# A decoder layer whose whole down projection goes by seven half-size products, with partial sums kept in PSUM or added in DRAM

## The chip, the cores and the metric

The kernel runs on one core of a Trainium2 chip. The metric is the device time of one execution in microseconds (us), in fp32, with inputs and outputs in DRAM. TensorE (PE) multiplies, VectorE (DVE) and ScalarE (ACT) do the rest of the arithmetic, GpSimd (POOL) only issues DMAs here, and SyncE (SP) issues most of the DMAs.

## The reference

One decoder layer over 512 tokens of width 2048: a mixer (attention heads beside a state-space scan), a cross-attention and an MLP, each with a residual. What the change touches is the last line and, through the weights' buffers, everything from `w_out` on:

```python
x = x + jnp.concatenate([attn, ssm], axis=-1) @ w_out[i]
x = x + cross_attention(rms_norm(x, g_cross[i]), rms_norm(mem, g_mem[i]), ...)
hm = rms_norm(x, g_mlp[i])
x = x + jnp.square(jax.nn.relu(hm @ w_up[i])) @ w_down[i]     # 2048 -> 8192 -> 2048
```

## The kernel before

Every large product is made of three TensorE products of a reduced fp32 type: each operand is split into a high part (an ACT copy) and a low part (a DVE subtraction), and high by high, high by low and low by high are added in PSUM. `weights` (L203 on) splits a plain 512 KB weight block; it takes 24 matmuls of 512 columns.

The up projection uses a scheme with seven products of half-size blocks in place of eight (Winograd's form). `up_forms` (L894) makes from one 512 KB block three raw quarters and four sums (DVE, L901 to L904), splits all seven (ACT L899 and L905, DVE L908 and L909); `forms` (L855) does the like for the activations. `up_products` (L916) runs 42 matmuls of 256 columns for such a block, into four PSUM banks, and `combine` (L924) makes the four result blocks from the seven sums. `up_out` (L941) applies the squared ReLU and writes the hidden rows to DRAM (`adr`).

The down projection goes over the 8192 hidden rows in NC = 8 chunks of 1024. In each chunk the first DS = 1024 output columns go by seven products (four column blocks S0 to S3 of 256, two weight blocks each), the other 1024 plainly (P0 and P1 of 512, four weight blocks each): 16 steps in a chunk, half of either kind. `mm_step` (L1089) takes four fresh banks for each column block, from the tags "mm" and "aux" in turn (eight banks in all), so that one block is emptied while the next is multiplied. `evac_step` (L1108) empties them: plain blocks by DVE into `acc` in SBUF (L1117), seven-product blocks by an ACT copy in the first chunk (L1130) and DVE additions after that (L1128), into `accs` in SBUF. `a_load`, `a_split` and `a_forms` (L1132 to L1145) load hidden rows and make their forms; `cols_sum` and `cols_out` (L1147 on) combine at the end, transpose on PE (L1158), add the residual `x3d` from DRAM (L1159) and store.

Order: from the mixer's end to L1050 parts are in an order written by hand; the up and down loops are placed by the compiler's scheduler, by priority in program order. Each engine and each DMA queue runs its own list in order. SBUF: the pool `wp` holds three raw weight blocks (WR) and two high and two low ones (WH) for the whole kernel; the mixer's scratch pool `bq` (12 tiles of 2 KB a partition, written by `ssd`, L589) is closed at L663, and `wq` (sums and their splits) opened on its bytes; 68 general tiles of 2 KB (`big`) hold activations. The first product after the mixer is `gemm_rows(cat, wout[0])` (called behind L682), whose first eight activation tiles are the attention's, ready before the last `ssd`.

## Time and profile before

| | us |
|---|---|
| median of 3 runs | 2353.99 (2353.25 to 2354.26) |
| profiled execution, whole | 2353.13 |
| its span, first to last instruction | 2351.1 |
| PE busy in the span | 2338.1 (99%) |
| DVE / ACT / POOL busy | 1686.9 / 1118.5 / 13.4 |

By place in the span: the mixer to about 690 us, the output projection to 906, cross-attention to 1015, the up projection from there to about 1667, the down projection to the end. A row of a group of instructions gives busy time, the mean duration of one in ns, and the idle time of its engine just before them with what ended it. Durations overlap by some 0.08 us from one instruction to the next on DVE and by more on PE; what an instruction costs in a full engine is the distance between starts.

### The profile page before, as it was taken

To read this page: it belongs to the slowest core of one execution; us is meant where nothing else is said; L and a number is where in the kernel's file an instruction comes from. 1 tells how busy PE (TensorE), PEld (TensorE's weight loads), DVE (VectorE), ACT (ScalarE), POOL (GpSimd) and SP (SyncE) were. 2 spreads that over 40 slices of the span, in tenths; PEclk is the share of its full clock that TensorE was granted. 3 is DMA by queue.
4 is the path that set the end of the run, shared out by engine and by line. 5 is a ranking of instruction groups with operands and counts; after the bars stand their busy time and mean duration, and the time that the engine had idled before them with its cause. 6 is when DMAs were issued, how large, how long until landed. Compare 5 with 4: busy or idle time off the path is not lost.

```text
span 2351.1 us, 36723 instructions
## 1 busy us (share of the span) xinstructions
PE 2338.1 (99%) x14606; PEld 2077.8 (88%) x14606; DVE 1686.9 (72%) x3100; ACT 1118.5 (48%) x1722; POOL 13.4 (1%) x30
## 2 busy tenths in 40 slices
PE   9999999999999999999999999999999999999999
PEld 8889977777778887789999999999988989889898
DVE  7544276686673346688888888888867887887787
ACT  6334277655452346675444444554543443443332
POOL 0000000000000000000000000000000000000000
PEclk9999999999999999999999999999999999999999
DMA  5222321122224456434443444444543433343344
GB/s 198 90 87 80 99 66 59 54 72 81 74 81 133 160 167 202 135 108 135 133 128 129 132 135 135 131 131 135 187 137 119 140 127 109 132 135 119 117 135 144
DMA packets 98283, 286.22 MB, mean 122 GB/s; under 512 B 11200, under 2 KB 15424, under 8 KB 98112
## 3 DMA queue, kind: packets, MB, share of 16 engines
q1 hardware_dynamic: 82368, 252.42, 33.3%
q10 hardware_dynamic: 13824, 25.17, 2.8%
q0 software_dynamic: 1920, 6.29, 0.9%
q8 instruction: 114, 1.87, 0.3%
q14 instruction: 57, 0.47, 0.1%
HBM read 254.48 MB, written 29.36 MB: 121 GB/s over the span
## 4 chain that ended last, share of the span: by engine, by line
PE 95%; ACT 2%; DVE 2%; issue 1%; DMA 0%; SPq 0%; ACTq 0%; DVEq 0%
PE mm L214 13%; PE mm L212 13%; PE mm L213 13%; PE aux L922 7%; PE mm L922 7%; PE aux L920 7%; PE mm L920 7%; PE aux L921 7%; PE mm L921 7%; PE aux L213 3%; PE aux L214 3%; PE aux L212 3%; PE aux L248 1%; PE aux L523 1%; PE aux L514 1%
## 5 line engine op out<-in xcount | busy, mean ns | idle before, releaser
L208 DVE TENSOR_TENSOR wl<-wr,wh 128x1024 fp32r<-128x1024 f32 (+2 forms) x223 | 264.4, 1186 | 281.7 <-ACT wh L207 280.9
L207 ACT ACTIVATE wh<-wr 128x1024 fp32r<-128x1024 f32 (+2 forms) x223 | 229.3, 1028 | 458.3 <-PE mm L214 250.3
L212 PE MATMUL mm<-wh,b 128*128 128x512 f32 (+2 forms) x1056 | 404.8, 384 | 3.3 <-ACT b L422 1.6
L213 PE MATMUL mm<-wl,b 128*128 128x512 f32 (+2 forms) x1056 | 402.8, 382 | 0.9 <-DVE wl L208 0.7
L214 PE MATMUL mm<-wh,b 128*128 128x512 f32 (+2 forms) x1056 | 402.6, 381 | 0.0
L899 ACT ACTIVATE wh<-wr 128x768 fp32r<-128x768 f32 x192 | 162.5, 846 | 309.4 <-PE mm L921 121.4
L909 DVE TENSOR_TENSOR sl<-sw,sh 128x1024 fp32r<-128x1024 f32 x192 | 234.5, 1221 | 97.1 <-ACT sh L905 96.8
L905 ACT ACTIVATE sh<-sw 128x1024 fp32r<-128x1024 f32 x192 | 203.6, 1061 | 120.3 <-DVE sw L904 37.1
L212 PEld LDWEIGHTS mm<-wh,b 128*128 128x128 f32 x1056 | 198.7, 188 | 42.9 <-ACT b L422 2.0
L213 PEld LDWEIGHTS mm<-wl,b 128*128 128x128 f32 x1056 | 198.8, 188 | 39.8 <-DVE wl L208 2.1
L214 PEld LDWEIGHTS mm<-wh,b 128*128 128x128 f32 x1056 | 198.7, 188 | 38.1 <-issue 0.2
L921 PE MATMUL mm<-b,sh 128*128 128x256 f32 x768 | 217.2, 283 | 0.0
L921 PE MATMUL aux<-b,sh 128*128 128x256 f32 x768 | 217.2, 283 | 0.0
L920 PE MATMUL mm<-b,sh 128*128 128x256 f32 x768 | 217.2, 283 | 0.0
L920 PE MATMUL aux<-b,sh 128*128 128x256 f32 x768 | 217.2, 283 | 0.0
L922 PE MATMUL mm<-b,sl 128*128 128x256 f32 x768 | 216.9, 283 | 0.0
L922 PE MATMUL aux<-b,sl 128*128 128x256 f32 x768 | 216.6, 283 | 0.0
L908 DVE TENSOR_TENSOR wl<-wr,wh 128x768 fp32r<-128x768 f32 x192 | 183.3, 955 | 26.9 <-ACT wh L899 19.8
L922 PE MATMUL aux<-b,wl 128*128 128x256 f32 x576 | 162.1, 282 | 1.2 <-DVE wl L908 1.1
L920 PE MATMUL mm<-b,wh 128*128 128x256 f32 x576 | 162.4, 282 | 0.0
L920 PE MATMUL aux<-b,wh 128*128 128x256 f32 x576 | 162.2, 282 | 0.0
L922 PE MATMUL mm<-b,wl 128*128 128x256 f32 x576 | 162.1, 281 | 0.0
(303 smaller groups left out, 5252.2 us busy)
## 6 DMA issues: line engine op xcount, KB each, us to landing
wr<-in_wup_dram SPq DMA_DIRECT2D x128, 512.0 KB, 3.8
wr<-in_wdp_dram SPq DMA_DIRECT2D x64, 512.0 KB, 3.7
wr<-in_wds_dram SPq DMA_DIRECT2D x64, 512.0 KB, 3.7
wr<-in_wzx_dram SPq DMA_DIRECT2D x48, 512.0 KB, 3.6
wr<-in_wout_dram SPq DMA_DIRECT2D x32, 512.0 KB, 3.8
a<-b ACTq DMA_DIRECT2D x64, 256.0 KB, 4.6
b<-a SPq DMA_DIRECT2D x64, 256.0 KB, 4.4
wr<-in_wqk_dram SPq DMA_DIRECT2D x31, 512.0 KB, 3.6
```

Of the source, the lines that this page charges most:

```text
L207: act.activation(hi, raw, AF.Copy)
L208: dve.tensor_tensor(lo, raw, hi.bitcast(F32), OP.subtract)
L212: pe.matmul(ps, l[0], r[0], start=start, stop=False)
L213: pe.matmul(ps, l[0], r[1], start=False, stop=False)
L214: pe.matmul(ps, l[1], r[0], start=False, stop=stop)
L899: act.activation(hi[:, :768], raw[:, 256:], AF.Copy)
L905: act.activation(shi, sw, AF.Copy)
L908: dve.tensor_tensor(lo[:, :768], raw[:, 256:], hi[:, :768].bitcast(F32), OP.subtract)
L909: dve.tensor_tensor(slo, sw, shi.bitcast(F32), OP.subtract)
L920: pe.matmul(ps[b][:, H], w[0][:, d], xf[0], start=st, stop=False, skip_group_check=True)
L921: pe.matmul(ps[b][:, H], w[0][:, d], xf[1], start=False, stop=False, skip_group_check=True)
L922: pe.matmul(ps[b][:, H], w[1][:, d], xf[0], start=False, stop=sp_, skip_group_check=True)
```

## The change

All 2048 columns of the down projection go by seven products: eight column blocks j of 256, two steps each, 16 steps in a chunk as before. Odd chunks take the columns in the reverse order; the last two blocks of a chunk stay in PSUM and go on in the next chunk. The other finished blocks are copied to SBUF by ACT, and DMAs from POOL write them to DRAM (`accd`), from the second time on with an addition there; for the last chunk they are loaded back (`acc_load`) and combined, and the last two blocks (LATE) are added on DVE. The residual is written straight to `out`, and the results are added to it there by DMAs from POOL. The seven sums are made with other signs, of the weights in three DVE instructions for four; in `up_products` the three products with raw quarters come first. The last two blocks of the up projection are interleaved. Weight buffers of the mixer (`wp`) are closed with it, and a pool `zp` is opened behind it, with four raw blocks.

```diff
-    wp = ctx.enter_context(tc.tile_pool(name="wp", bufs=2))
...
     bq = mixer.enter_context(tc.tile_pool(name="bq", bufs=NBUFQ))
+    wp = mixer.enter_context(tc.tile_pool(name="wp", bufs=2))
+    weight_tile = {"raw": lambda: wp.tile([128, 1024], F32, name="wr", tag="wr", bufs=WR), ...
...
     mixer.close()
-    wq = ctx.enter_context(tc.tile_pool(name="wq", bufs=WQ, reuse_waits="tile"))
+    zp = ctx.enter_context(tc.tile_pool(name="zp", bufs=2, reuse_waits="tile"))
+    weight_tile.update(raw=lambda: zp.tile([128, 1024], F32, name="zr", tag="zr", bufs=WZ),
+                       hi=lambda: zp.tile([128, 1024], F32R, name="zh", tag="zh", bufs=WH),
+                       lo=lambda: zp.tile([128, 1024], F32R, name="zl", tag="zl", bufs=WH))
...
-            act.dma_start(x3d[t, n], xr[t])
+            act.dma_start(out[t * 128:t * 128 + 128, n * 512:n * 512 + 512], xr[t])
...
+    prods = ((5, 4, 0, H0), (6, 5, 1, H0), (4, 0, 3, H0), (3, 3, 2, H0), (2, 2, 2, H1), (1, 1, 1, H1), (0, 6, 0, H1))
...
+        sw = zp.tile([128, 1024], F32, name="sw", tag="sw", bufs=WH)
+        rhi = zp.tile([128, 768], F32R, name="rh", tag="rh", bufs=WH)
+        rlo = zp.tile([128, 768], F32R, name="rl", tag="rl", bufs=WH)
+        shi, slo = weight_tile["hi"](), weight_tile["lo"]()
...
+        act.activation(rhi, q(raw, 0, 3), AF.Copy)
+        dve.tensor_tensor(h3(q(sw, 2, 2), 2), h3(q(raw, 0, 2), 2), q(raw, 3)[:, None, :].to_broadcast([128, 2, 256]), OP.add)
+        dve.tensor_tensor(q(sw, 1), q(sw, 2), q(raw, 1), OP.add)
+        dve.tensor_tensor(q(sw, 0), q(sw, 1), q(raw, 2), OP.add)
+        dve.tensor_tensor(rlo, q(raw, 0, 3), rhi.bitcast(F32), OP.subtract)
+        act.activation(shi, sw, AF.Copy)
+        dve.tensor_tensor(slo, sw, shi.bitcast(F32), OP.subtract)
...
+        for part in (prods[:3], prods[3:]):
+            for d in range(2):
+                for wi, xi, b, H in part:
...
+        dve.tensor_tensor(h3(t1, 2), h3(b[1], 2), p1[:, None, :].to_broadcast([128, 2, 256]), OP.add)
+        dve.tensor_tensor(h3(t2, 2), h3(b[2], 2), t1[:, None, H1].to_broadcast([128, 2, 256]), OP.add)
+        dve.tensor_tensor(t1[:, H1], b[0][:, H1], t2[:, H1], OP.add)
+        stt_(t3[:, H0], t2[:, H0], b[2][:, H1])
+        stt_(t3[:, H1], t2[:, H0], b[3][:, H0])
...
+    steps = [("U", 0, f, q, 4) for q in range(4) for f in (NU - 2, NU - 1)]
+    US = len(steps)
+    js = [list(range(NJ))[::1 - c % 2 * 2] for c in range(NC)]
+    steps += [("S", c, j, q, FCH // 512) for c in range(NC) for j in js[c] for q in range(FCH // 512)]
+    stays = {(c, j) for c in range(NC - 1) for j in js[c][-2:]}
...
+        fresh = q == 0 and (c - 1, j) not in stays
+        if fresh:
             tags[0] += 1
-            banks[kind, c, j] = [bank("mm" if tags[0] % 2 else "aux") for _ in range(4)]
+            banks[kind, j] = [bank("mm" if tags[0] % 2 else "aux") for _ in range(4)]
...
+            for b, w in enumerate(BW):
+                o = big()
+                act.activation(o[:, w], ps[b][:, w], AF.Copy)
+                if j in written:
+                    nc.gpsimd.dma_start(accd[j][b], o[:, w], accum_op=OP.add)
                 else:
-                    act.activation(accs[j][b][:, w], ps[b][:, w], AF.Copy)
+                    nc.gpsimd.dma_start(accd[j][b], o[:, w])
...
+        dve.tensor_tensor(h3(f1, 2), h3(ta, 2), tb[:, None, H1].to_broadcast([128, 2, 256]), OP.subtract)
+        stt_(f2[:, H0], f1[:, H0], ta[:, H1])
+        stt_(f2[:, H1], f2[:, H0], tb[:, H0])
+        a, b, f, g = split(ta), split(tb[:, H0], 256), split(f1), split(f2)
...
+            for k, o in enumerate((a, b)):
+                pe.transpose(p[:, 256 * i + 128 * k:256 * i + 128 * k + 128], o, ident)
+            act.activation(r[:, h], p[:, h], AF.Copy, scale=c2[:, t:t + 1])
+            nc.gpsimd.dma_start(out[t * 128:t * 128 + 128, j * 256:j * 256 + 256], r[:, h], accum_op=OP.add)
...
+        for p, (l, f) in enumerate(((-6, -4), (-5, -3), (-3, -1), (-2, 0)) if c == 0 else ((-15, -14), (-12, -11), (-9, -8), (-6, -5))):
+            task(b + l, a_load, c, p)
+            task(b + f, a_forms, c, p)
...
+        load_step(i + WZ - 1)
+        prep_step(i + 1)
+        if 0 < i <= len(steps):
             evac_step(i - 1)
+        for t in tasks.get(i, ()):
+            t[0](*t[1:])
+        if i < len(steps):
             mm_step(i)
...
-WR, WH, WQ = 3, 2, 2
+WR, WH, WZ = 3, 2, 4
+LATE = 2
```

## Rows read from the trace of the kernel before

**Rows 1.** The page: busy time of each engine, its share, its instructions.
```profile
PE 2338.1 (99%) x14606; PEld 2077.8 (88%) x14606; DVE 1686.9 (72%) x3100; ACT 1118.5 (48%) x1722; POOL 13.4 (1%) x30
```

**Rows 2.** Stretches: length, busy PE, PEld, DVE, ACT, POOL; clock, DMA share, GB/s.
```profile
1080.00:1640.00 560.00, 560.00 (x4707) 560.00 (x4706) 466.98 (x869) 279.77 (x365) 0.00 (x0) 1.00 0.41 132
1859.53:1944.20 84.67, 84.67 (x531) 76.22 (x530) 66.59 (x113) 32.70 (x40) 0.00 (x0) 1.00 0.39 125
663.00:694.75 31.75, 29.86 (x167) 21.66 (x165) 25.05 (x48) 19.64 (x39) 0.00 (x0) 1.00 0.21 68
```

**Rows 3.** Chain that ended last, last pieces: start, us, what.
```profile
2339.60 1.23 PE mm L1158 x10
2347.13 0.75 DVE b L1117
```

**Rows 4.** Instructions by line, PE, 663 to 694.75 us: busy, mean ns, idle before.
```profile
L212 PE MATMUL mm<-wh,b 128*128 128x512 f32 x29 | 12.2, 433 | 1.7 <-ACT wh L207 0.9 <-ACT b L186 0.8
L214 PE MATMUL mm<-wh,b 128*128 128x512 f32 x28 | 11.2, 402 | 0.0
L213 PE MATMUL mm<-wl,b 128*128 128x512 f32 x28 | 11.1, 398 | 0.2 <-DVE wl L208 0.2
```

**Rows 5.** Timeline around the mixer's end, several engines: start, us, instruction.
```profile
663.25 30.69 SPq L199 DMA_DIRECT2D wr<-in_wout_dram  x5
685.68 0.48 PE L644 MATMUL aux<-q 128*64 128x128 f32 x3
694.75 0.50 PE L212 MATMUL mm<-wh,b 128*128 128x512 f32 x1 [0.78 <-ACT b L186]
```

**Rows 6.** The page, DMA issues: KB each, median us to landing; and queue 1.
```profile
wr<-in_wout_dram SPq DMA_DIRECT2D x32, 512.0 KB, 3.8
b<-x2d POOLq DMA_DIRECT2D x16, 256.0 KB, 4.1
b<-x3d SPq DMA_DIRECT2D x16, 128.0 KB, 3.5
out_dram<-b SPq DMA_DIRECT2D x16, 128.0 KB, 2.0
q1 hardware_dynamic: 82368, 252.42, 33.3%
```

**Rows 7.** Timeline of DVE: distances between starts at three widths.
```profile
700.07 3.69 DVE L187 TENSOR_TENSOR b<-b 128x512 fp32r<-128x512 f32 x6
2320.44 1.23 DVE L208 TENSOR_TENSOR wl<-wr,wh 128x1024 fp32r<-128x1024 f32 x1
2321.58 1.02 DVE L1128 TENSOR_TENSOR b<-mm,b 128x512 f32<-128x512 f32 x2
2324.10 0.42 DVE L936 TENSOR_TENSOR b<-b 128x256 f32<-128x256 f32 x1
2324.43 0.42 DVE L937 TENSOR_TENSOR b<-b 128x256 f32<-128x256 f32 x1
```

**Rows 8.** Instructions by line, DVE and ACT, 1700 to 2300 us.
```profile
L908 DVE TENSOR_TENSOR wl<-wr,wh 128x768 fp32r<-128x768 f32 x57 | 54.2, 950 | 8.6 <-ACT wh L899 8.6
L905 ACT ACTIVATE sh<-sw 128x1024 fp32r<-128x1024 f32 x58 | 61.5, 1060 | 44.8 <-DVE sw L904 31.4 <-PE mm L921 8.3 <-PE aux L921 4.2
L899 ACT ACTIVATE wh<-wr 128x768 fp32r<-128x768 f32 x58 | 49.1, 846 | 134.9 <-PE aux L214 40.7 <-PE mm L921 37.9 <-PE mm L214 26.1
L1130 ACT ACTIVATE b<-mm 128x512 f32<-128x512 f32 x6 | 3.5, 594 | 5.9 <-PE mm L922 5.9
L1130 ACT ACTIVATE b<-mm 128x256 f32<-128x256 f32 x2 | 0.8, 396 | 0.0
```

**Rows 9.** Timeline of POOL: three issues in a row.
```profile
906.16 1.60 POOL L868 DMA_DIRECT2D b<-x2d  x3 [24.57 <-PE mm L214]
```

**Rows 10.** Timeline of the end: the last stores and the last matmul.
```profile
2345.11 3.13 SPq L1120 DMA_DIRECT2D out_dram<-b  x3
2346.70 0.40 PE L214 MATMUL aux<-wh,b 128*128 128x512 f32 x1
```

More of the change, by code (lines that the diff above doesn't have):

```diff
@@ L123, in tile_layer @@
     bq = mixer.enter_context(tc.tile_pool(name="bq", bufs=NBUFQ))
+    wp = mixer.enter_context(tc.tile_pool(name="wp", bufs=2))
+    weight_tile = {"raw": lambda: wp.tile([128, 1024], F32, name="wr", tag="wr", bufs=WR),
+                   "hi": lambda: wp.tile([128, 1024], F32R, name="wh", tag="wh", bufs=WH),
+                   "lo": lambda: wp.tile([128, 1024], F32R, name="wl", tag="wl", bufs=WH)}
     def big(dtype=F32):
@@ L197, in load @@
         a, n = src.shape[1], src.shape[2]
-        raw = wp.tile([128, 1024], F32, name="wr", tag="wr", bufs=WR)[:, :a * n]
+        raw = weight_tile["raw"]()[:, :a * n]
         nc.sync.dma_start(h3(raw, a), src)
@@ L259, in tile_layer @@
     pos_i = cp.tile([128, 4], I32, name="pos_i")
-    first = wp.tile([128, 1024], F32, name="wr", tag="wr", bufs=WR)
+    first = weight_tile["raw"]()
     ahead.append((first, 2, 1024))
@@ L278, in split_h @@
         if i == 0:
-            hi = wp.tile([128, 1024], F32R, name="wh", tag="wh", bufs=WH)
-            lo = wp.tile([128, 1024], F32R, name="wl", tag="wl", bufs=WH)
+            hi = weight_tile["hi"]()
+            lo = weight_tile["lo"]()
             ahead[0] = h3(hi, 2), h3(lo, 2)
@@ L671, in tile_layer @@
     x2d = dp.tile([4, 4, 128, 512], F32, name="x2d")
-    x3d = dp.tile([4, 4, 128, 512], F32, name="x3d")
     def residual(b, ps, t, n, ss_, dst):
@@ L894, in up_forms @@
     def up_forms(raw):
-        w21, w11, w12, w22 = (raw[:, 256 * i:256 * i + 256] for i in range(4))
-        hi = wp.tile([128, 1024], F32R, name="wh", tag="wh", bufs=WH)
-        sw = wq.tile([128, 1024], F32, name="sw", tag="sw")
-        shi = wq.tile([128, 1024], F32R, name="sh", tag="sh")
-        act.activation(hi[:, :768], raw[:, 256:], AF.Copy)
-        s1, s2, s3, s4 = (sw[:, 256 * i:256 * i + 256] for i in range(4))
-        dve.tensor_tensor(s1, w21, w22, OP.add)
-        dve.tensor_tensor(s2, s1, w11, OP.subtract)
@@ L1079, in load_step @@
             kind, c, j, q, n = steps[i]
-            if kind == "P":
-                raws[i] = load(wdp[j, c * n + q])
-            else:
-                raws[i] = up_weights(j, c * n + q, wup if kind == "U" else wds)
+            raws[i] = up_weights(j, c * n + q, wup if kind == "U" else wdn)
     def prep_step(i):
         if i < len(steps):
-            wts[i] = weights(raws.pop(i)) if steps[i][0] == "P" else up_forms(raws.pop(i))
+            wts[i] = up_forms(raws.pop(i))
     def mm_step(i):
@@ new lines, in tile_layer @@
+    last = US + per * (NC - 1)
+    for i, j in enumerate(js[-1]):
+        end = last + 2 * i + 2
+        if i < NJ - LATE:
+            task(end + 2, acc_load, j)
+            task(end + 3, cols_sum, j)
+            task(end + 4, cols_out, j, 0)
+            task(end + 5, cols_out, j, 1)
+        else:
+            task(end - 2, acc_load, j)
+            task(end + 1, cols_sum, j)
+            task(end + 1, cols_out, j, 0)
+            task(end + 1, cols_out, j, 1)
+    for i in range(WZ - 1):
+        load_step(i)
```

227 lines of the change are left out of this document (82 added, 145 removed).

## The prediction

> **What bounds the kernel now.** I read the busy times first: PE is busy for 2338.1 of 2351.1 us [rows 1]. Busy matmuls overlap, so this alone doesn't say that PE sets the pace; the stretches do. In the up projection and in a down chunk PE has no gap at all, at a granted clock of 1.00 (the upper of its two levels), while DVE is busy 466.98 of 560.00 us and 66.59 of 84.67 us, ACT far less, and the DMA engines 0.41 and 0.39 of the time [rows 2]. The chain of waits ends with PE work and a last DVE step [rows 3]. So each matmul taken out of the down projection is worth its issue time, and each gap that opens on PE costs its whole length: nothing later has slack to give it back. DVE is the nearest second, at 83% and 79%.
>
> **Products.** Per step of seven products PE runs 42 matmuls of 256 columns; at 560.00 us for 4707 [rows 2] one costs 0.119 us, so a step 5.00 us. A chunk of 8 plain and 8 such steps takes 84.67 us [rows 2] (528 matmuls are programmed, the row counts 531 with its edges), so a plain step is (84.67 - 39.97) / 8 = 5.59 us. The change turns 64 plain steps into seven-product steps: 64 x 0.59 = **-37.7 us**. That is 10%, not the eighth that the scheme saves in columns, because a 256-column matmul costs more than half a 512-column one.
>
> **Transposes.** The 1024 further columns come out transposed: 32 more PE transposes. Ten cost 1.23 us [rows 3], so 0.123 each. Eight fall into the tail below, 24 are in the body: **+3.0 us**.
>
> **The mixer's end.** This part of the diff looks like bookkeeping and is the largest cost that I see. Before, the weight buffers outlive the mixer: the loads of `w_out` are issued from about 663 us [rows 5], while the last two `ssd` still run, and PE fills the waits of `ssd` with the first output block, whose attention half needs no `ssd`. Between 663 and 694.75 us it runs 29 + 28 + 28 = 85 of its matmuls [rows 4], at 5.59 / 24 = 0.233 us each 19.8 us of work. Behind the change these weights go into `zp`. `bq` (12 x 2 KB) and `wp` (7 x 4 KB) make 52 KB, and so does `zp` (4 x 4, 4 x 4, 2 x 4, 4 x 3 KB): it lies on their bytes, its raw tiles first, on eight of the twelve scratch tiles. `ssd` takes seven scratch tiles a call, and the last ones are read by the matmuls of L644 until 686.2 us [rows 5]. I find no raw tile that is likely to be free of them, so the load comes behind the last `ssd`; 3.8 us to landing [rows 6], an ACT conversion of about 1.06 us (as L905) [rows 8], and the first product is some 5 us behind it. Without the filling matmuls `ssd` itself should end earlier, at 681 to 686 us: DVE, busy 25.05 of 31.75 us there [rows 2], bounds that. So output starts at 686 to 692 us, needs 19.8 us to reach where it stood at 694.75, and is 11 to 17 us late; I take **+14**. The ends: 0 (a free tile; weights ready in time) and 20 (all of the filling lost). SP has only these loads and those of `x` behind the wait.
>
> **DVE in the down projection.** DVE's distance between starts is 0.615 us for 512 columns (six in 3.69), 1.14 for 1024 and 0.33 for 256 [rows 7]; 768 columns, with a row of 0.950 [rows 8], about 0.87. A step after the change: 0.615 + 2 x 0.335 + 0.87 + 1.14 = 3.30 us. Forms of one pair of hidden rows: 4 x 0.615 + 3 x 0.335 = 3.46 us, four pairs a chunk. A chunk: 16 x 3.30 + 13.8 = 66.6 us against 16 x 5.00 = 80 us of PE: still 83%, as in the up projection, where PE has no gap; in the stretches with forms (three steps a pair) 13.4 of 15 us. DVE's former additions (L1128) go away to ACT, which has for a chunk 16 x (0.85 + 1.06) + 6 x 2.2 + about 9 us of forms = 53 of 80 us [rows 8]. I cost the steady state at 0; its cover is the distance of DVE from 100%. In the up projection each block gets fewer DVE instructions, under a PE that is full: 0. **Entry**: the plain steps, light on DVE, used to cover the first forms of the down projection. Now the nine steps around the seam hold 9 x 3.30 + 13.8 + 2 combinations of 2.2 = 48 us of DVE in 45 us of PE: 3 us over, 5 if the third combination counts, 0 if two sets of buffers absorb it. **+3** (0 to 5).
>
> **The turns.** Six fresh blocks a chunk is an even number, so after each of seven turns the third block's tag is that of the block just finished: its banks can't be filled before ACT has emptied them, three copies of 0.594 and one of 0.396, 2.2 us [rows 8]. Bank 3 ends with the first part of the products, so it is free early; bank 2 and 1 end 0.7 and 0.36 us before the last matmul. A fresh block that takes the banks in the order in which they come free waits some 0.5 us; if all copies start after the last matmul, with sequencing, some 2.2 us. Behind the copies on ACT stands the conversion of the next weights (1.06 us), with a step of lead. 7 x 0.5 = **+3.5** (0 to 15). The page Perfetto Trace Analysis of the Trainium skill, section Matmuls, says that independent groups should rotate through different banks so that emptying one overlaps the next group's products; the change breaks this at the turns alone, and by that rule the turns cost the upper end, 15.
>
> **Partial sums by DMA.** An evacuation writes 3 x 0.262 + 0.131 = 0.917 MB, six a chunk. POOL takes 0.53 us to issue one DMA (three in 1.60) [rows 9], 24 a chunk: hidden. Nothing in the trace adds in DRAM. Plain traffic moves 252.42 MB in 33.3% of the span, 0.322 MB a us [rows 6]. A chunk's weights and hidden rows, 10.5 MB, take 33 of 80 us; 5.5 MB more cost 17 us if an addition moves as a plain store, 34 if the old sums are read as well: 50 to 67 of 80 us. Hidden, at 0; the 68 general tiles hold two chunks' forms (64) and one evacuation (4). In the last chunk a load waits on SP for an addition to land; behind it stand weight loads, three steps (15 us) ahead. The former SP loads of `x3d` and stores go away, hidden before.
>
> **Tail.** Before, the last matmul ends at 2347.1 us, then one DVE step, one store [rows 3, 10] and the end at 2351.1: 4.0 us. After: one DVE addition (0.68), a combination (2.2), four transposes (0.6), four ACT copies (1.6), a POOL issue (0.5), and a landing between 2.0 (a store of this size) and 5.5 (a load and a store); I take 4.1, what POOL's loads take [rows 6]. 9.7 us, so **+6** (3.5 to 8.5).
>
> **Sum** against the profiled execution, 2353.1 us: -37.7 + 3.0 + 14 + 3 + 3.5 + 6 = -8.2, 2344.9. The median of the runs lies 0.9 us above that execution: **2346 us**.
>
> **Rivals.** (a) The boundary is hidden: the raw tile that comes first is one that `ssd` no longer reads, and the loads run ahead. For it: a tile waits only for users of its own bytes. Against: seven of twelve tiles are the last call's. -14: 2332. (b) The turns cost their upper end: 2346 + 11.5 = 2357.5, no change. (c) Slower: adding in DRAM runs at half of a plain transfer's rate or less, so the DMA engines become the bound of a chunk. From 11 MB in 80 - 33 = 47 us on, 0.23 MB a us, it decides; at 0.161 a chunk takes 33 + 68 = 101 us, seven chunks 147 us more, 2490; a little past the threshold gives 2360 to 2400. For it: no row shows such a DMA. Against: 0.39 of the DMA time in use [rows 2]. The page Collectives: The Full Stack, section on the bandwidth ceiling, says that an addition in the DMA datapath costs not the arithmetic but a second source read, which is the 34 us above; that page speaks for hidden, and no row here shows it. (d) The products bring less than the sum, because in stretches with forms DVE (13.4 of 15 us) waits on ACT and PE on DVE: 1 us a pair, 28 pairs, 2374.
>
> **How the numbers follow.** Forecast 0.46 (2336 to 2356), (a) 0.21, (b) 0.15, (c) 0.10, (d) 0.08. A measurement of this kernel can tell about 0.2%, 4.7 us: faster is below 2349.3. Faster: 0.33 of the forecast's 0.46, all of (a), 0.02 of (b): 0.56. Same: 0.12 + 0.11 = 0.23. Slower: 0.01 + 0.02 + 0.10 + 0.08 = 0.21. Range: low end 2332 less entry and turns, 2326; high end 2346 + 6 (boundary) + 12 (turns) = 2364; beyond it lie (c) and most of (d).
>
> **What would show it.** Right: no PE gap in a chunk but some tenths at each third block; a chunk of 80 us; a PE gap of over 10 us in sum between 663 and 695 us, ended by ACT's conversion of the first `zr`; end 10 us behind the last matmul. Wrong: loads of `w_out` before the last `ssd` (a); gaps of 2 us ended by ACT copies (b); SP loads landing late and POOL's DMAs queued up (c); PE waiting on DVE's low parts in mid-chunk (d). The forecast fails altogether if the granted clock falls to its lower level in the gap at the mixer's end; no row shows that level, so I give it no term.

## The result, and the profile after

| kernel | median, us | runs, us | ratio to before |
|---|---|---|---|
| before | 2353.88 | 2353.25 to 2354.26 | |
| changed | 2373.35 | 2370.22 to 2374.23 | 1.0081 (95% interval 1.0063 to 1.0098) |

The change makes the kernel 0.8% slower. The forecast was 2346, faster, with a range that ended at 2364: wrong in sign and outside the range. The span of the profiled execution went from 2351.1 to 2372.4 us, so 21.3 us have to be found, and 29.5 against the forecast's -8.2.

The page of the changed kernel: busy times, to set beside [rows 1], and the queue q0, which moved 6.29 MB in 0.9% of the time before:

```profile
PE 2315.2 (98%) x15790; PEld 2129.2 (90%) x15790; DVE 1712.1 (72%) x2896; ACT 1246.4 (53%) x1994; POOL 198.5 (8%) x254
...
q0 software_dynamic: 31872, 54.54, 13.3%
```

PE has 23 us less to do, and the span is 21 us longer: 57 us without PE work in place of 13. Stretches of the changed kernel, with the columns of [rows 2]: the mixer's end, 40 us inside one block of `w_out`, 400 us of the up projection, a down chunk from its first to the next one's first product, the last chunk, and the tail behind the last product.

```profile
660.00:690.00 30.00, 17.10 (x88) 12.30 (x89) 19.39 (x41) 16.13 (x34) 0.00 (x0) 0.66 0.21 76
735.00:775.00 40.00, 40.00 (x179) 33.11 (x178) 11.94 (x13) 9.13 (x11) 0.00 (x0) 1.00 0.36 119
1130.00:1530.00 400.00, 400.00 (x3336) 400.00 (x3335) 323.44 (x498) 197.44 (x258) 0.00 (x0) 1.00 0.39 131
1844.40:1926.90 82.50, 80.94 (x675) 80.73 (x674) 69.37 (x108) 48.03 (x72) 20.99 (x24) 1.00 0.83 195
2256.70:2353.90 97.20, 89.78 (x715) 87.95 (x713) 68.17 (x106) 46.42 (x73) 38.32 (x44) 0.96 0.93 220
2353.90:2372.40 18.50, 3.87 (x23) 2.44 (x23) 4.94 (x11) 4.81 (x12) 10.55 (x12) 0.71 0.68 85
```

Three of these rows show idle PE: 12.9 us at the mixer's end, 7.4 in the last chunk, 14.6 in the tail; there the granted clock is a mix of its two levels, 0.66, 0.96 and 0.71. The chunk has 1.56 us of idle PE. Two more rows show something that no idle time gives away: in the up projection PE is as full as before, yet 400 us hold 3336 instructions, one each 0.1199 us, where [rows 2] gave 0.119; and in a block of `w_out` PE gets through more of them than before. The same two stretches of the kernel before:

```profile
724.00:764.00 40.00, 40.00 (x174) 32.44 (x173) 11.02 (x12) 8.22 (x9) 0.00 (x0) 1.00 0.35 117
1130.00:1530.00 400.00, 400.00 (x3363) 400.00 (x3362) 333.66 (x621) 199.92 (x261) 0.00 (x0) 1.00 0.41 132
```

What PE, DVE and SP waited for in the changed kernel (us in total, times, longest; each line from the list of waits of the stretch that the text names):

```profile
PE aux L640 <- DVE q L632: 9.4, 4, 3.8
...
PE mm L925 <- ACT b L1112: 11.0, 7, 1.6
PE mm L1152 <- DVE b L850: 3.1, 1, 3.1
PE aux L1152 <- DVE b L850: 2.5, 1, 2.5
...
DVE b L936 <- DMA b<-acc: 9.9, 3, 5.1
...
SPq L1138 <- DMA acc<-b: 16.1, 12, 5.7
```

The first is from 660 to 690 us: PE stands inside `ssd`, with nothing to fill its waits. The second, from 1750 to 2354 us, is the seven turns. The rest is the last chunk: SP's loads of the old sums (L1138) wait for additions in DRAM, DVE (L936) for those loads, and the output's transposes (L1152) for DVE, with the next products behind them on PE.

With the starts of PE's matmuls as marks, the 21.3 us lie as follows (the rows add up to 21.5, by rounding):

| where | forecast | measured |
|---|---|---|
| mixer, up to 655 us | 0 | -5.1 |
| mixer's end | +14 | +16.9 |
| `w_out` to the first up product | 0 | -4.9 |
| up projection | 0 | +3.8 |
| products of the down projection | -37.7 | -32.2 |
| seven turns | +3.5 | +12.7 |
| entry, transposes and the last chunk | +6.0 | +15.8 |
| tail | +6.0 | +14.5 |

How the marks give these: the same matmuls start 5.1 us earlier than before up to 655 us and 11.7 later behind the boundary; the first up product stands at 1027.73 for 1020.96, the first down product at 1676.25 for 1665.71, the last product ends at 2353.88 for 2347.1. A chunk of sixteen seven-product steps would be 80.64 without a turn (experiment 2), so the products are 8 x (84.67 - 80.64). Seven chunks carry 1.82 us over that. The first chunk is 5.1 us over it and the last 14.7 more; of the old down projection 4.0 us lay outside its eight times 84.67, which is taken off.

### The profile page after: what moved, and what is told of

The parts are those of the page before. It is cut to its first block, busy times and chain, and to the rows that moved or that the text cites. A ratio compares the mean times of both kernels' runs of the same rounds, so it can differ in the third digit from the quotient of the medians.

```text
span 2372.4 us, 40157 instructions
## 1 busy us (share of the span) xinstructions
PE 2315.2 (98%) x15790; PEld 2129.2 (90%) x15790; DVE 1712.1 (72%) x2896; ACT 1246.4 (53%) x1994; POOL 198.5 (8%) x254
## 5 line engine op out<-in xcount | busy, mean ns | idle before, releaser
L910 ACT ACTIVATE zh<-sw 128x1024 fp32r<-128x1024 f32 x256 | 271.2, 1059 | 373.4 <-PE aux L926 150.8
L911 DVE TENSOR_TENSOR zl<-sw,zh 128x1024 fp32r<-128x1024 f32 x256 | 313.2, 1224 | 170.5 <-ACT zh L910 169.4
L926 PE MATMUL mm<-b,zh 128*128 128x256 f32 x1024 | 290.3, 284 | 1.0 <-DVE b L187 1.0
L925 PE MATMUL mm<-b,zh 128*128 128x256 f32 x1024 | 290.5, 284 | 0.0
L925 PE MATMUL aux<-b,zh 128*128 128x256 f32 x1024 | 290.2, 284 | 0.0
L927 PE MATMUL mm<-b,zl 128*128 128x256 f32 x1024 | 290.1, 283 | 0.0
L926 PE MATMUL aux<-b,zh 128*128 128x256 f32 x1024 | 289.9, 283 | 0.0
L927 PE MATMUL aux<-b,zl 128*128 128x256 f32 x1024 | 289.3, 283 | 0.0
L909 DVE TENSOR_TENSOR rl<-zr,rh 128x768 fp32r<-128x768 f32 x256 | 244.0, 953 | 14.5 <-ACT rh L905 10.7
L925 PE MATMUL mm<-b,rh 128*128 128x256 f32 x768 | 218.4, 285 | 11.0 <-ACT b L1112 11.0
L926 PE MATMUL mm<-b,rh 128*128 128x256 f32 x768 | 217.9, 284 | 1.5 <-DVE b L187 1.5
L925 PE MATMUL aux<-b,rh 128*128 128x256 f32 x768 | 218.7, 285 | 0.0
L926 PE MATMUL aux<-b,rh 128*128 128x256 f32 x768 | 218.1, 284 | 0.0
L926 PEld LDWEIGHTS mm<-b,zh 128*128 128x128 f32 x1024 | 196.8, 192 | 1.2 <-DVE b L187 1.2
L925 PEld LDWEIGHTS mm<-b,zh 128*128 128x128 f32 x1024 | 196.6, 192 | 0.0
```

The lines of the kernel that those rows point to most:

```text
L909: dve.tensor_tensor(rlo, q(raw, 0, 3), rhi.bitcast(F32), OP.subtract)
L910: act.activation(shi, sw, AF.Copy)
L911: dve.tensor_tensor(slo, sw, shi.bitcast(F32), OP.subtract)
L925: pe.matmul(ps[b][:, H], w[0][:, d], xf[0], start=st, stop=False, skip_group_check=True)
L926: pe.matmul(ps[b][:, H], w[0][:, d], xf[1], start=False, stop=False, skip_group_check=True)
L927: pe.matmul(ps[b][:, H], w[1][:, d], xf[0], start=False, stop=sp_, skip_group_check=True)
```

## The experiments

All times are medians beside runs of the kernel before on the same chip, whose medians lay between 2353.7 and 2354.7 us. A gain is against the changed kernel's 2373.35.

**1. The weight pool outlives the mixer again.**

```
     cp = ctx.enter_context(tc.tile_pool(name="cp", bufs=1))
+    wp = ctx.enter_context(tc.tile_pool(name="wp", bufs=2))
...
-    wp = mixer.enter_context(tc.tile_pool(name="wp", bufs=2))
...
-    weight_tile.update(raw=lambda: zp.tile(...), hi=..., lo=...)
...
-WR, WH, WZ = 3, 2, 4
+WR, WH, WZ = 3, 2, 3
```

> The changed kernel, with its raw and rounded weight tiles in a pool that outlives the mixer, as in the kernel before; only the summed tiles and the forms change place at the mixer's end (and three raw tiles in place of four). Theory of separate local causes: the gap of TensorE at the mixer's end goes (busy 17.1 us of the 30 from 660 to 690 becomes over 25), the granted clock there stays at 1.00, the 768th product of w_out moves back by 6 to 8 us; and since the raw weights' rounded halves now lie where they lay before, a 256-column matmul that takes its weights from them may return from 0.1200 to 0.118 us: some 4 us in the up and 5 in the down projection. Sum 2373.35 - 7 = 2366 without that, 2357 with it. Rival (the DMA additions of the down projection are behind the loss): the end moves by at most the 7 us of the boundary, and the matmul interval stays at 0.1200. A third view, that the boundary's loss is won back later anyway: 2372 to 2374.

2359.0 us, a gain of 14.4. Stretches of this kernel, the mixer's end and the up projection:

```profile
660.00:690.00 30.00, 28.88 (x166) 21.50 (x165) 26.84 (x51) 17.94 (x35) 0.00 (x0) 1.00 0.21 69
1130.00:1530.00 400.00, 400.00 (x3362) 400.00 (x3362) 325.33 (x501) 199.36 (x260) 0.00 (x0) 1.00 0.38 132
```

The gap at the mixer's end is gone, the clock is 1.00 there, and 400 us hold 3362 matmuls again: sixteen steps take 80.00 us, not 80.64. Yet the first up product comes only 4.9 us earlier, since the 10 us that the changed kernel had gained around its boundary are lost as well. So the pool's place does two things, and one is no wait at all.

**2. A fresh pair takes the bank set opposite to the last step's.**

```
-            tags[0] += 1
-            banks[kind, j] = [bank("mm" if tags[0] % 2 else "aux") for _ in range(4)]
+            setof[kind, j] = "mm" if cur[0] == "aux" else "aux"
+            banks[kind, j] = [bank(setof[kind, j]) for _ in range(4)]
+        cur[0] = setof[kind, j]
```

> The changed kernel, with a fresh pair of the down projection put into the bank set opposite to the one that the step before it wrote (so at a turn the new pair's banks were read out two blocks ago). Theory of separate local causes: the stall of 1.85 us in each of the seven chunks (first product of a block that waits for ScalarE's read of the same banks, 1.56, and some 0.3 behind it) goes: chunks of 82.4 become 80.6, 2373.35 - 13 = 2360. Rival (load of the DMA engines): a stall that is only seen at the turn, but comes from work late through full DMA queues, stays in another place: 2369 to 2374.

2363.0 us, a gain of 10.4. One chunk of this kernel, first to next first product:

```profile
2082.60:2163.20 80.60, 80.60 (x674) 80.60 (x673) 69.27 (x108) 47.90 (x72) 20.98 (x24) 1.00 0.84 200
```

PE has no gap, with 24 additions in DRAM in the stretch and the DMA engines at 0.84. Six chunks in a row take 80.64 us, as sixteen up steps do: neither the additions nor DVE hold PE up, and the turn alone was the 1.82 us. Seven turns are 12.7 us, and the gain is 10.4: the last chunk took part of it back, 99.0 us for 97.2, with longer waits of PE's transposes for DVE.

**3. The residual added by VectorE, all stores on SP.**

```
-            act.dma_start(out[...], xr[t])
+            act.dma_start(x3d[t, n], xr[t])
...
+            nc.sync.dma_start(r[:, h], x3d[...])
-            act.activation(r[:, h], p[:, h], AF.Copy, scale=c2[:, t:t + 1])
-            nc.gpsimd.dma_start(out[...], r[:, h], accum_op=OP.add)
+            dve.scalar_tensor_tensor(r[:, h], p[:, h], c2[:, t:t + 1], r[:, h], op0=OP.mult, op1=OP.add)
+            nc.sync.dma_start(out[...], r[:, h])
```

> The changed kernel, with the residual x2 kept in a DRAM tile of its own; the end loads it back on SP, VectorE adds it to the scaled transpose, and SP stores to the output: no addition in DRAM at the output, and no GpSimd issue in the tail. Theory of separate local causes: of the tail of 18.5 us between the last product's end and the span's end the twelve serial issues of 0.85 us (10.55 us) go and the landing falls to that of a store; the tail becomes 7 to 9 us, 2373.35 - 10 = 2363. Rival (load of the DMA engines): the tail waits for additions of partial sums that are queued ahead on the same engines; plain stores wait behind them too, and 2370 to 2374 stays.

2391.5 us: 18 slower, which neither theory had. Waits of SP and of PE in its last chunk:

```profile
SPq L1156 <- DVE b L1155: 13.4, 8, 6.7
...
PE mm L1154 <- DVE b L1155: 9.8, 3, 4.6
```

The stores (L1156) wait on SP for VectorE, and what is queued behind them (residuals, old sums, weights) goes out only after them. The last chunk took 107.1 us for 97.2, and the tail became 26.0 us. The run says nothing on GpSimd's part in the tail. That the queue, with waiting stores ahead of loads, made the loss, and not VectorE's additions themselves, is argued from these waits and not shown. The edit was made again below, with the loads ahead.

**4. The last chunk's old sums loaded ahead, all eight.**

```
-LATE = 2
+LATE = 8
```

> The changed kernel, with the last chunk's old sums of all eight pairs (not of the last two) loaded ahead of the chunk's end and added by VectorE from PSUM: no addition in DRAM and no way back from it in the last chunk. Theory: the last chunk's 14.7 us over the others is 3.0 of transposes and 11 to 12 of late reloads (VectorE waits 5.12 us for one, TensorE stands 2.81 and 3.35 us) and the granted clock of 0.83 behind these; both go: 2373.35 - 10 = 2363 (2361 to 2367, as the tail is as before). Rival: the last chunk is slow since VectorE has 32 sums to make from PSUM there, which this kernel adds to: 2373 to 2380.

2361.3 us, a gain of 12.1. The last chunk of this kernel:

```profile
2256.90:2346.90 90.00, 89.59 (x730) 86.91 (x728) 79.53 (x134) 39.40 (x57) 24.38 (x28) 1.00 0.70 173
```

PE is full, the clock 1.00, and the chunk 90.0 us for 97.2, though DVE does 11 us more: the wait was for the old sums on their way through DRAM, not for work of DVE. What is left over 82.46 is about the price of its 56 transposes (0.123 each by [rows 3], 6.9 us). The tail fell as well, to 12.6 us; four issues of POOL stand in it, where the changed kernel has twelve.

**5. The last two pairs' output without an addition in DRAM** (experiment 3 for these alone, the residual loaded with the old sums, two blocks ahead).

```
+        if j // 2 in X3:                                  # in acc_load; X3 = (0,)
+            res[j] = [big(), big()]
+            ... nc.sync.dma_start(res[j][t // 2][...], x3d[t, j // 2, ...])
```

> The changed kernel, with the output of the last two pairs (columns 0 to 511) made without an addition in DRAM: their residual is kept in a DRAM tile, loaded on SP together with the pairs' old sums, two blocks ahead, added by VectorE from PSUM, and stored by SP. The other six pairs stay as they are. It replaces the run that loaded each residual just before its use and put all stores on SP: there the loads and stores stood on SP's queue ahead of the old sums that the next pair waits for. Theory (the tail of 18.5 us is GpSimd's serial issue of additions of 0.85 us and their landing of 6 us): the tail falls to 8 to 11 us, 2373.35 - 9 = 2364 (2362 to 2367). Rival (the tail is the additions of the pairs before, that the stores wait behind on the DMA engines): 2370 or more.

2369.7 us, a gain of 3.6 where the theory had 9; the tail is 14.0 us for 18.5, and not 8 to 11. So part of the tail is the additions to the output; four more of them, of the pair before, still stand in it (POOL's timeline, from 2355.70 us on). In the changed kernel POOL, in the timeline of the end, issues twelve of them in a row, and the list of DMA issues gives how long additions take to land:

```profile
2356.44 10.55 POOL L1154 DMA_DIRECT2D out_dram<-b  x12 [4.35 <-ACT b L1153]
```
```profile
acc<-b POOLq DMA_DIRECT2D x144, 256.0 KB, 6.1
...
out_dram<-b POOLq DMA_DIRECT2D x32, 128.0 KB, 6.6
```

That is 0.88 us an issue, where [rows 9] gave 0.53 for a load, and 6.6 us to landing, where a store of that size, issued by SP, took 2.0 [rows 6].

**6. Partial sums stored, not added.**

```
-                    nc.gpsimd.dma_start(accd[j][b], o[:, w], accum_op=OP.add)
+                    nc.gpsimd.dma_start(accd[j][b], o[:, w])
```

> The changed kernel, with every store of a partial sum a plain store in place of an addition in DRAM. It leaves out the sums over the chunks for the pairs that are evicted: the output holds only the last part of each. Theory of separate local causes: the additions are hidden in the chunks, which stay at 82.46 us; only the last chunk may gain, where loads wait for the last additions: 2366 to 2374. Rival (the load of the DMA engines, on which an addition weighs as a further read): the chunks fall toward 80.64, the granted clock's dips of the last chunk go, 2345 to 2360.

2366.5 us, in one run. 80 us of a chunk of this kernel and of the changed one, with 24 issues on POOL in each:

```profile
2088.00:2168.00 80.00, 78.44 (x653) 78.23 (x653) 67.81 (x105) 47.47 (x72) 12.79 (x24) 1.00 0.57 199
```
```profile
2091.80:2171.80 80.00, 78.43 (x654) 78.23 (x653) 67.28 (x105) 47.48 (x72) 21.02 (x24) 1.00 0.86 201
```

PE's row is the same to 0.01 us, and chunks stay at 82.46. An addition costs POOL 0.88 us in place of 0.53, and the DMA engines 0.29 of 80 us, 23 us a chunk, at the same bytes a second: hidden. Only the last chunk shortens, 97.2 to 88.8. What DVE's first combination waits for there, where the changed kernel had 9.9 us:

```profile
DVE b L936 <- DMA b<-acc: 1.5, 3, 0.6
```

No transpose waits for DVE there any more, though the sums still go to DRAM and come back. So in the last chunk it is the addition that made them late, and not the way through DRAM as such; one run shows it.

**7. Three edits together** (1, 2 and 4).

> The changed kernel with three of the single edits together: raw and rounded weights in a pool that outlives the mixer, fresh pairs in the bank set opposite to the last step's, and all eight old sums of the last chunk loaded ahead. Theory of separate local causes: the single gains add up, 14.4 + 10.4 + 12.1 = 36.9 off 2373.35 = 2336.5 (2333 to 2341), 0.75% under the kernel before. Rival (one shared cause, the load of the DMA engines, that each edit relieves a little): less than 25 us in all, 2348 or more.

2336.5 us, ratio 0.9923 (0.9902 to 0.9944). The single gains 14.4 + 10.4 + 12.1 make 36.9; the three together brought 36.8, far from the rival's 25 or less, so the causes are separate. That they agree to 0.1 us is luck: the four runs of experiment 2 alone lie between 2360.1 and 2366.2.

**8. 640 unused bytes between the streamed tiles and the weights.** In the kernel before the rounded raw quarters began 448 bytes past a multiple of 1024, the streamed tiles at 832; the changed kernel has both at 832.

```
+    pad = ctx.enter_context(tc.tile_pool(name="pad", bufs=1))
+    nc.gpsimd.memset(pad.tile([128, 160], F32, name="pad"), 0.0)
     mixer = ExitStack()
```

> The changed kernel, with 640 bytes a partition of unused SBUF ahead of the mixer's pools: nothing else changes, but every weight tile begins 448 bytes past a multiple of 1024, while the tiles that the matmuls stream stay at 832. In the kernel before the raw quarters lay at 448 (0.1178 us a matmul) and the sums at 832 (0.1200); in the changed one all lie at 832; in the run with the outliving pool the sums' halves lie at 448 (0.1184) and the raw ones at 832 (0.1200). Theory (the place relative to the streamed tile, modulo 1024, sets the interval): all 42 matmuls of a step come to about 0.1178, a step falls from 5.04 to about 4.95 us, sixteen from 80.64 to 79.2, and 256 steps give 23 us: 2373.35 - 23 = 2350 (2347 to 2353). Rival (what counts is that the weights lie in the lower part of SBUF, under 64 KB): nothing changes, 80.64 stays, 2371 to 2375.

2373.2 us, no change in the median, and yet the theory was half right. Stretches of this kernel, 40 us inside a block of `w_out` and the up projection, against the changed kernel's 179 and 3336:

```profile
743.00:783.00 40.00, 40.00 (x174) 32.43 (x173) 11.02 (x12) 8.87 (x10) 0.00 (x0) 1.00 0.35 119
1130.00:1530.00 400.00, 400.00 (x3373) 400.00 (x3373) 326.15 (x503) 200.65 (x264) 0.00 (x0) 1.00 0.38 133
```

256-column matmuls became faster, 0.1187 us (sixteen steps 79.75 us), 512-column ones slower: a block of 192 takes 44.47 us from its first start to its last, as before the change, and 43.41 in the changed kernel; over its 191 steps from start to start that is 0.2328 and 0.2273 each. The first up product came at 1040.75, 13 us later than in the changed kernel: the 10 us of the 512-column matmuls, and a boundary that cost 19.5. From there on it was won back at 0.9 us in sixteen steps.

**9. 640 bytes ahead of everything, and 512 bytes in place of 640.**

```
+    pad = ...
+    nc.gpsimd.memset(pad.tile([128, 160], F32, name="pad"), 0.0)
     cp = ctx.enter_context(tc.tile_pool(name="cp", bufs=1))
```


> The changed kernel, with 640 bytes of unused SBUF ahead of all tiles: weights and streamed tiles alike now begin at 448 modulo 1024. Theory (the place of the weights relative to the streamed tiles sets the interval of matmuls): nothing changes against the changed kernel, 0.2268 us for a 512-column matmul of w_out, 80.64 us for sixteen steps, 2370 to 2375. Rival (the weights' own place, 448 or 832, sets it): 0.2325 us and 79.75 us as with the pad behind the streamed tiles, first up product at 1040 in place of 1028 us.


```
+    pad = ...
+    nc.gpsimd.memset(pad.tile([128, 128], F32, name="pad"), 0.0)
     mixer = ExitStack()
```


> The changed kernel, with 512 bytes of unused SBUF ahead of the mixer's pools in place of 640: the weights begin at 320 modulo 1024, the streamed tiles at 832, 512 bytes apart. With no shift a 512-column matmul of w_out took 0.2268 us and sixteen steps 80.64 us; with 640 bytes 0.2325 and 79.75. Theory that only a whole number of 512 bytes counts: as with no shift, 2370 to 2375. Theory that any shift within 1024 bytes acts alike: as with 640, the first up product near 1040 and sixteen steps near 79.75.

2375.3 and 2375.0 us, in one run each. In this order, a block of `w_out` and the up projection:

```profile
736.00:776.00 40.00, 40.00 (x178) 33.12 (x177) 11.48 (x12) 9.13 (x12) 0.00 (x0) 1.00 0.37 119
1130.00:1530.00 400.00, 400.00 (x3336) 400.00 (x3335) 323.74 (x499) 197.83 (x259) 0.00 (x0) 1.00 0.38 131
```
```profile
736.00:776.00 40.00, 40.00 (x179) 33.10 (x178) 11.94 (x13) 9.13 (x11) 0.00 (x0) 1.00 0.35 119
1130.00:1530.00 400.00, 400.00 (x3336) 400.00 (x3334) 323.73 (x499) 198.32 (x259) 0.00 (x0) 1.00 0.38 131
```

Both are the changed kernel's rates. So it is not where the weights lie, but how far they lie from the tiles of the other operand, and a whole number of 512 bytes counts as none.

**10. The kernel before, with the pools' boundary alone.**

```
-    wp = ctx.enter_context(tc.tile_pool(name="wp", bufs=2))
+    W = {"p": mixer.enter_context(tc.tile_pool(name="wp", bufs=2))}
...
     mixer.close()
+    W["p"] = ctx.enter_context(tc.tile_pool(name="zp", bufs=2, reuse_waits="tile"))
```

> The kernel before, with one thing of the change: its weight pool is closed with the mixer and opened anew over the freed bytes, as the changed kernel does. The cost of the mixer's end alone: the 768th product of w_out comes 6 to 8 us later, with TensorE idle for over 10 us between 660 and 690 and a granted clock under 0.8 there. Beside that all its weight tiles then lie at 832 modulo 1024 as the streamed ones do. Theory (place sets the interval): sixteen up steps take 80.64 instead of 80.00, some 0.04 us for each of the 192 half-size steps (+7.7) and the same share in the plain products; 2354.1 + 6 + 8 = 2368 (2364 to 2372). Rival (the interval has another cause in the changed kernel): 80.00 stays, 2354.1 + 6 = 2360 or less, down to 2354 where the boundary's loss is won back.

2360.0 us, ratio 1.0023 (1.0012 to 1.0034): slower by 5.8, where 14 were expected. The boundary and the up projection of this kernel:

```profile
660.00:690.00 30.00, 17.85 (x82) 12.51 (x82) 18.08 (x39) 14.52 (x31) 0.00 (x0) 0.56 0.15 53
1130.00:1530.00 400.00, 399.48 (x3329) 399.28 (x3329) 329.79 (x613) 198.78 (x259) 0.00 (x0) 1.00 0.41 131
```

The time alone would have spoken for the rival (2360 or less). Yet all the parts are there: 18.8 us at the boundary, 80.64 us for sixteen steps, 43.4 for a block of `w_out`. The last had the wrong sign in the expectation ("the same share in the plain products"): before and after the boundary, and in the plain steps of the down projection too (a chunk with its eight plain steps takes 83.88 for 84.67), the 512-column matmuls give much of the loss back.

**11. Four edits, and five.** The three of experiment 7 with the output of all eight pairs without an addition in DRAM, and this with the pad of experiment 8 ahead of the mixer's pools, which moves the raw quarters' rounded halves to another distance.

> The changed kernel with the three edits that added up to 2336.5 us, and for all eight pairs the output without an addition in DRAM: the residual kept in a DRAM tile, loaded on SP with the old sums, two blocks ahead. Theory (the rest of the tail, 12.5 us there, is the last four serial GpSimd issues and the landing of the last addition): the tail falls by the 4.5 us that the last two pairs gave alone, 2336.5 - 4.5 = 2332 (2329 to 2334). Rival (VectorE, which takes up another 32 additions of 0.48 us in the last chunk and the old sums there, becomes the bound of the last chunk): 2335 to 2342.

> The kernel with four edits, and 640 bytes a partition of unused SBUF behind the streamed tiles: with it the raw quarters' rounded halves (18 of the 42 matmuls of a step) begin 448 bytes past a multiple of 1024 as the sums' halves do, and no longer at 832 as the streamed tiles. Theory (place relative to the streamed tile): the step falls from 5.000 to 4.984 us as in the run with the pad alone, 256 steps give 4 us: 2328 (2326 to 2331) if four edits give 2332. Rival (no effect with the outliving pool): the same as four edits, within 1 us.

2339.0 and 2332.2 us (ratio 0.9914, 0.9898 to 0.9931). The first is 2.4 slower than with three edits, less than its runs scatter; but in the profiled executions its tail is 9.8 us for 12.5 and its last chunk 98.1 for 89.2. The last chunk of four edits, and the waits of PE and of DVE in it:

```profile
2231.00:2329.00 98.00, 89.42 (x730) 87.81 (x728) 90.76 (x164) 27.67 (x29) 0.00 (x0) 0.98 0.67 214
```
```profile
PE aux L1156 <- DVE b L937: 3.2, 3, 1.5
PE mm L1156 <- DVE b L937: 2.9, 2, 1.5
PE aux L1156 <- DVE b L935: 2.5, 1, 2.5
...
DVE sw L905 <- DMA wr<-in_wdn_dram: 7.3, 2, 4.1
```

DVE is busy 90.76 of 98 us, and all of PE's waits end with it, as the rival had it. But what DVE is not busy it waits, 7.3 us, for weight loads; these stand on SP among stores that wait for DVE (26.1 us of such waits), so how much of the 9 us is DVE's work and how much the queue, this run does not separate. With the pad, sixteen steps take 79.75 us as expected, 6.7 us in the median in place of 4; the last chunk, 5.3 us shorter, adds to it, which no expectation had.

**12. The same with the output of the last two pairs only, and with two distances.** In the second the rounded halves of all but the up and down projections begin 384 bytes further on, a whole number of 512 bytes from the streamed tiles.

```
-   "hi": lambda: wp.tile([128, 1024], F32R, name="wh", ...),
+   "hi": lambda: wp.tile([128, 1152], F32R, name="wh", ...)[:, 96:1120],      # "lo" alike
...
-        shi, slo = weight_tile["hi"](), weight_tile["lo"]()
+        shi, slo = [wp.tile([128, 1152], F32R, name=n, ...)[:, :1024] for n in ("wh", "wl")]
-NBUF = 68
+NBUF = 67
```

> The kernel with five edits, without the second place of the weight halves. It is the run with four edits and the pad, but with the output made without additions in DRAM only for the last two pairs, not for all eight. Theory (with all eight, VectorE was the bound of the last chunk: its 32 additions from PSUM took 9 us there): the last chunk is as with three edits, 89 us, the tail 8 to 9.8 us: 2336.5 - 4 - 3 = 2329.5 (2327 to 2332). Rival (the last chunk's loss had to do with loads of the residual on SP, which stay in part): 2332 or more.

> The kernel with five edits (outliving pool, opposite bank sets, all old sums of the last chunk loaded ahead, output of the last two pairs without an addition in DRAM, 640 unused bytes), in which moreover the rounded weight halves of everything but the up and down projections begin 384 bytes further on, which puts them a whole number of 512 bytes from the streamed tiles (one streamed tile fewer, for the room). Theory (the distance of the operands' places modulo 512 sets the interval, and it goes the other way for 512 columns than for 256): the 512-column matmuls of the mixer and of w_out fall from 0.2325 to 0.227 or 0.228 us, the first up product comes from 1021.5 to 1011 us, the up and down steps stay at 4.984 us: 10 us under the same kernel without it, 2319 (2316 to 2322). Rival (the 10 us gained in the changed kernel are the boundary's own, work that it lets run ahead): 0.2325 stays or the first up product stays at 1021, no difference.

2328.2 us (0.9898, 0.9883 to 0.9913) and 2317.0 us (0.9849, 0.9836 to 0.9861). Stretches of the first and then of the second kernel, a block of `w_out` and the up projection:

```profile
725.00:765.00 40.00, 40.00 (x174) 32.46 (x173) 10.91 (x11) 9.22 (x11) 0.00 (x0) 1.00 0.34 119
1130.00:1530.00 400.00, 400.00 (x3373) 400.00 (x3372) 326.13 (x503) 199.54 (x261) 0.00 (x0) 1.00 0.38 132
```
```profile
718.00:758.00 40.00, 40.00 (x178) 33.17 (x177) 11.94 (x13) 9.13 (x11) 0.00 (x0) 1.00 0.34 119
1130.00:1530.00 400.00, 400.00 (x3373) 400.00 (x3373) 325.87 (x501) 199.63 (x261) 0.00 (x0) 1.00 0.38 133
```

The first up product comes at 1011.05 for 1022.90 us, with no boundary in either kernel. So the 10 us of the changed kernel are the distance of the operands, not work that its boundary lets run ahead. The second kernel is 1.5% faster than the one before, with the change's products in it. In the first the last chunk takes 89.7 us, as with three edits, so additions by DVE for two pairs alone cost little there.

**13. The copies of a turn ahead of the next forms.**

```
-        prep_step(i + 1)
         if 0 < i <= len(steps):
             evac_step(i - 1)
+        prep_step(i + 1)
```

> The changed kernel, with the copies that empty a finished pair's banks put ahead of the next step's weight forms in program order, so that on ScalarE the conversion of the next sums (1.06 us) no longer stands between a block's last matmul and the first copy. Theory (the order on ScalarE's queue makes the turn's stall): the stall falls from 1.82 us by the conversion to about 0.8, a chunk of 82.46 to 81.4 us, 2373.35 - 7 = 2366 (2364 to 2368). First rival (the stall is the copies' own, all four of them): 82.46 and 2372 to 2375 stay. Second rival (the conversions, now behind four copies that wait for the block's end, make each of the 48 blocks late): chunks of over 83 us, 2378 or more.

2373.6 us, stalls as before. It tells nothing of its question: the compiler's scheduler sets the order on each engine, and on ScalarE it came out the same but for one place. A turn in the changed kernel, timeline of ScalarE (start, us, what):

```profile
2112.09 1.06 ACT L910 ACTIVATE zh<-sw 128x1024 fp32r<-128x1024 f32 x1 [0.99 <-ACT b L186]
2113.06 1.83 ACT L1112 ACTIVATE b<-mm 128x512 f32<-128x512 f32 x4
```

The block's last matmul starts at 2111.84, the next block's first at 2113.69, when the first of four copies is done. The conversion L910 stands ahead of them. That it makes 1.06 of the 1.82 us is read from these rows, not shown by a run.

## Why the prediction was wrong

**What bounds the kernel: right.** The gaps on PE cost about their length: experiment 7 brought the sum of the single gains. A little was given back in experiment 2 alone, whose last chunk grew by 1.8 us.

**Products: right in kind, 5.5 us short.** The term took 0.119 us for each of the 42 matmuls of a step from [rows 2]. That was a mean over two kinds: those with raw quarters at 0.1178, those with sums at 0.1200. The change moved all weights to the sums' distance, so all take 0.1200, and a chunk is 80.64 us, not 80.0. The same costs 3.8 us in the up projection, which the prediction put at 0 because PE is full there and DVE has less to do. It read a stable duration as a property of the shape.

**The mixer's end: right, +16.9 for +14.** The steps of the term are in the timeline around it (several engines: start, us, what):

```profile
681.04 0.84 PE L644 MATMUL aux<-q 128*64 128x128 f32 x3
...
681.10 15.04 SPq L199 DMA_DIRECT2D zr<-in_wout_dram  x7
...
684.86 1.06 ACT L207 ACTIVATE zh<-zr 128x1024 fp32r<-128x1024 f32 x1 [0.80 <-DMA zr<-in_wout_dram]
...
685.97 0.79 PE L212 MATMUL mm<-zh,b 128*128 128x512 f32 x1
```

The load goes out 0.06 us after the first of the last three matmuls that read `ssd`'s scratch, 18 us later than in [rows 5], and the first product follows after 4.9 us, at the early end of "686 to 692". Rival (a) falls. Two details were off: the idle time is not in one gap before ACT's first conversion but in `ssd`'s own waits on DVE (9.4 us), which the missing products had filled; and the granted clock, given no term, is 0.66 from 660 to 690, against 1.00 with the pool that outlives the mixer. The lower level in this gap was the sign by which the forecast was to fail altogether; it came, and the term still lay within 3 us. How much of the 16.9 us is the clock, no run separates. The total hid this term: seen from the first up product only 6.8 us remained, and it took the runs with pads to show that the other 10 were a gain of another kind.

**Turns: mis-sized, 12.7 for 3.5.** The cause was named with its place and an upper end of 15; the value taken was wrong. The text had the conversion of the next weights behind the copies; the rows of experiment 13 show it ahead. It also had the new block take banks in the order in which they come free; in the trace the first product waits for a copy that starts only 1.2 us behind the start of the last matmul. Rival (b) was nearly this. By the rule of the Trainium skill that the prediction quoted (Perfetto Trace Analysis, section Matmuls: rotate banks, so that emptying one overlaps the next group) an unbroken rotation costs nothing. The trace agrees: experiment 2 restores the rotation, and its chunk has no gap on PE. The page gives no price for a broken one; the 15 was the prediction's own upper end, and 12.7 was measured.

**DMAs and DVE in the chunks: right.** Additions in DRAM are hidden (experiments 2 and 6), and chunks of 80.64 us with a full PE show that DVE does not hold it up. Rivals (c) and (d) fall for the chunks; that (d)'s time, 2374, lies next to the measured one is luck. The signs of (c), late loads on SP and additions queued on POOL, came in the last chunk and the tail alone. The estimate of "50 to 67 of 80 us" of DMA time came out at 69 (0.86 of 80). An addition costs 23 us a chunk over a plain store. The page Collectives: The Full Stack of the Trainium skill, in the section on the bandwidth ceiling, has such a price, for collectives, as a second source read; the prediction's estimate by it was 17, the half of 34, so the trace agrees in kind and is above it in size.

**The last chunk: the step that failed.** Here the mechanism was wrong and not only a size. The prediction wrote "In the last chunk a load waits on SP for an addition to land", noted 15 us of lead for the weight loads behind it, and gave it nothing; the further transposes got 3 us. It did not follow the reloaded sums: evicted, added, read back, combined and transposed in a chain in which an addition took 6.1 us to land and a load 5.9 (medians of the whole kernel), with the DMA engines busy 0.93 of the stretch. DVE then waited up to 5.1 us, and PE stood behind the transposes that need DVE. Experiment 4 takes that chain away, 7.2 us here; experiment 6 keeps it, with plain stores for the additions, and 8.3 us go. So what was put at nothing is the landing of the additions ahead of a reader. The rest of the 14.7 us is about the price of the chunk's 56 transposes, 6.9 us. The cover of DMAs that was right for a chunk without a reader was wrong for the one with a reader.

**Entry:** the first chunk takes 5.1 us over 80.64, where the term of +3 had 5 as its upper end; no run took it apart, and what the same place cost before is not separated.

**Tail: mis-sized, +14.5 for +6.** One POOL issue of 0.53 us and a landing of 4.1 were assumed. Twelve issues of 0.88 stand there, one behind the other, the output of three pairs and not of one, and their landing takes 6.2 (the median of the twelve). With no addition to the output left in it (experiments 11 and 12) the tail is 9.3 to 9.9 us, where the prediction had 9.7. Nothing in the trace of before added in DRAM, and the price was bounded by plain loads and stores, which lie below it.

**The range** left out that several terms could lean to one side together: rate, turns, last chunk, tail and boundary came out above by 3.8 + 5.5 + 9.2 + 9.8 + 8.5 + 2.9 = 39.7 us, and one gain of 10 was unforeseen.

## What to carry to other kernels

Before a pool is moved, note how far the weights lie from the tiles that they are multiplied with: here the distance moved the interval of the matmuls by 1.1% at 256 columns and 2.4% at 512, and a term worked out from a mean duration is only as good as the places behind it. When weights move onto freed bytes, look for what filled the gaps of the stage that frees them. A DMA that is hidden while nobody reads its result need not be hidden in the stage that does: follow the last one to its reader.

## What was not expected of the hardware

- In these runs the interval of back-to-back matmuls goes with the distance, modulo 512 bytes, between the places of the two operands in SBUF, the other way round for two widths. At none (0 or 512 bytes): 0.1200 us for 256 columns, 0.2273 for 512. At 640 (for 256 columns at 128 too, experiment 12): 0.1187 where all weights of a step lie so, 0.1178 and 0.1184 where only the raw quarters (before) or only the sums (experiment 1) do, and 0.2328 for 512 columns. Other distances were not tried, and why it turns round with the width stays open.
- An addition in DRAM issued by GpSimd took 0.85 to 0.88 us to issue for 0.53, and 6.1 us to land for a plain store's 3.5 (256 KB, the two kernels of experiment 6).
